# Where the sums of quarters for the two feed-forward output products are made

## The chip, the cores and the metric

The kernel runs on one core of a Trainium2 chip. The metric is device microseconds of that core, median of three runs. A core has five engines with a queue each, worked off in order: TensorE (PE in the profile; its weight loads are PEld), VectorE (DVE), ScalarE (ACT), GpSimd (POOL) and SyncE (SP), which here only issues transfers. A wait at the head of a queue holds everything behind it.

## The reference

Two transformer blocks run one after the other on a sequence of 1024 tokens of width 1024. Each ends with a feed-forward part, of which the part in question is the second product:

```python
# first block (D_FF = 3072), second block (FFN_HIDDEN = 2816)
x = x + (jax.nn.gelu(gate) * val) @ w_down[l]
x = x + (jax.nn.silu(gate) * up) @ w_ffn_out[l]
```

All is float32. The remaining parts (attention, recurrences, convolutions, norms, the first feed-forward products) are not touched.

## The kernel before

Activations are kept transposed, 128 channels on the partitions and 1024 tokens along the row. A float32 product is made of three matmuls on split operands, high by high, low by high and high by low (`mm3`, L389), where the high part is a rounded copy and the low part what the rounding left.

Each second product is computed by Strassen's scheme of seven half-size products. The hidden dimension is taken in pairs of 128 rows (12 pairs in the first block, 11 in the second); a pair has two weight tiles `wa`, `wb` and two activation tiles `ga`, `gb`, each 128x1024, loaded by SP from DRAM (`load`, L1837; all four show as `fs` in the profile). Every tile has a lower and an upper half. The seven products need sums and differences of halves, made in place or in the tiles `s` (weights) and `t` (activations): `sums` (L1846) writes `s1 = wa_lo - wa_hi`, `wa_hi += wb_hi`, `s0 = wa_hi - wa_lo`, `t1 = gb_hi - ga_hi`, `ga_hi -= ga_lo`, `t0 = gb_hi - ga_hi`, `t2 = gb_lo - t0`. An eighth, `s2 = wb_lo - s0`, is made later, in `down`'s inner function `operands`. All are TENSOR_TENSOR of 128x512 by the helper at L1542.

`down` (L1894) runs the work as a list of steps: groups of three pairs (the last group of the second block has two), within a group the seven products in turn, within a product the pairs. That gives 84 steps in the first block and 77 in the second. A step is 12 matmuls into four accumulator tiles `pd`. Three steps ahead of its matmuls a step's operands are prepared (`operands`, L1861): ScalarE rounds the weight half to `whi` (L384), writes `-whi` into `wlo` (L385), and a transfer issued by GpSimd adds the weight half to it (L386, `accum_op`); ScalarE rounds the activation half (L378) and VectorE subtracts (L379). The buffers `hi`/`lo` are four deep, so ScalarE starts on step x+3 when TensorE has left step x-1.

When the three pairs of a product are done, its four `pd` tiles are added to `acc` or to the residual tiles by VectorE (L1542, `add` L1872), two after the next step and two after the one behind that, before TensorE may use those accumulators again. The table `due` says behind which step the sums of a pair stand; a pair four ahead is loaded when its buffers come free. The engines' order is that of the code.

Of the kernel before, what the change touches and what calls it, by code (L numbers as in the profile page):

```python
# [16 lines left out]
ALU = mybir.AluOpType  # L17
# [3 lines left out]
S = 1024  # L21
# [3 lines left out]
H = 512  # L25
# [66 lines left out]
class Rope:  # L92
# [38 lines left out]
    def rstd(self, sums, n, post=None):  # L131

        nc, net = self.nc, self.net
        f = net.rt.unsqueeze(2).to_broadcast([P, 8, n])
        m = self.tp.tile([P, 8, n], F32, tag=f"qm{n}", name="qm")
        nc.vector.tensor_tensor(m, sums.rearrange("p (b n) -> p b n", n=n), f, op=ALU.mult)
        nc.vector.tensor_tensor(m, m, f, op=ALU.mult)
        r = net.rstd_small(m.rearrange("p b n -> p (b n)"), 8 * n, 1.0 / 64, EPS)
        rv = r.rearrange("p (b n) -> p b n", n=n)
        if post is None:  # L140
            nc.vector.tensor_tensor(rv, rv, f, op=ALU.mult)
        else:
            nc.vector.scalar_tensor_tensor(rv, rv, post, f, op0=ALU.mult, op1=ALU.mult)
        return r

    def sums(self, sq, n):
        pst = self.net.psT.tile([P, H], F32, tag="T", name="pst")
        self.net.colsum(pst, sq, self.net.ind[n], nb=8)
        return self.rstd(pst[:, 0:8 * n], n, 0.125 if n == 4 else None)
# [1373 lines left out]
class Ffn:  # L1523
# [17 lines left out]
    def tt(self, e, o, x, y, op=ALU.add):  # L1541
        e.tensor_tensor(o, x, y, op=op)  # L1542
# [303 lines left out]
    def sums(self, k):  # L1846

        t = self.raw[k]
        v, p, lo, hi = self.nc.vector, self.nc.gpsimd, slice(0, H), slice(H, S)
        sub = lambda e, o, x, y: self.tt(e, o, x, y, ALU.subtract)  # L1850
        t["s"], t["t"] = self.tile("s", k), self.tile("t", k)
        s, q, wa, wb, ga, gb = [t[n] for n in ("s", "t", "wa", "wb", "ga", "gb")]
        sub(v, s[:, 1], wa[:, lo], wa[:, hi])
        self.tt(p, wa[:, hi], wa[:, hi], wb[:, hi])
        sub(p, s[:, 0], wa[:, hi], wa[:, lo])
        sub(v, q[:, 1], gb[:, hi], ga[:, hi])
        sub(v, ga[:, hi], ga[:, hi], ga[:, lo])
        sub(v, q[:, 0], gb[:, hi], ga[:, hi])
        sub(v, q[:, 2], gb[:, lo], q[:, 0])

    def operands(self, i, k):  # L1861
        t, net = self.raw[k], self.net
# [23 lines left out]
    def down(self, dp, last, end):  # L1886
        nc, net = self.nc, self.net
        lo, hi = slice(0, H), slice(H, S)
# [29 lines left out]
        residual((0, 1, 2, 3))  # L1918
        self.load(3, "wa", "ga", "gb", "wb")
        due = [(0, 0), (1, 1), (2, 2), (9, 3)]  # L1920
        summed = set()

        def sums(k):
            if k not in summed:
                summed.add(k)
                self.sums(k)

        def operands(x):
            g, i, k = steps[x]
            if i not in (0, 2):  # L1930
                sums(k)
            self.operands(i, k)
            if i == (2 if g else 4):
                t = self.raw[k]
                self.tt(nc.gpsimd, t["s"][:, 2], t["wb"][:, lo], t["s"][:, 0], ALU.subtract)
            if k + 4 < n:
                if i == 4:
                    self.load(k + 4, "ga", "wa")
                elif i == orders[g][-1]:
                    self.load(k + 4, "gb", "wb")  # L1940
                    due.append((max(x - look + 2, due[-1][0] + 3 if due else 0), k + 4))

        for x in range(look):
            operands(x)
# [43 lines left out]
        for x, (g, i, k) in enumerate(steps[:len(steps) - rest]):  # L1988
            if g == len(groups) - 1 or g == 0 and i == 2:
                for f in adds:  # L1990
                    f()
                adds = []
            if x + look < len(steps):
                operands(x + look)
            for f in hooks.get(x - 0.5, ()):
                f()
            h, l = self.ready.pop(0)
            b, first = self.DOWN[i][4:]
            if k == groups[g][0] and first:
                banks[b] = [net.psB.tile([P, H], F32, tag="B", name="pd") for _ in range(4)]  # L2000
            for q in range(4):
                qs = slice(q * P, (q + 1) * P)
                net.mm3(banks[b][q], [((h[:, qs], l[:, qs]), (h[:, hi], l[:, hi]))],
                        first and k == groups[g][0], k == groups[g][-1], not first)
            for f in adds[:2]:
                f()
            del adds[:2]
            for f in hooks.get(x, ()):
                f()
            if due and due[0][0] <= x:  # L2010
                sums(due.pop(0)[1])
            if k == groups[g][-1]:
                for f in adds:
                    f()
                adds = self.add(banks[b], acc, g, i)
# [686 lines left out]
def ffn_plan(up, down, nf):  # L2702
    return pair_plan([up[i] for i in range(2 * nf)]) + [(f"sd{i}", down[i * P:(i + 1) * P, :]) for i in range(nf)]
# [149 lines left out]
```

## Time and profile before

| | us |
|---|---|
| median of three runs (3649.17 to 3652.49) | 3649.85 |
| the profiled execution | 3642.82 |
| its span, first to last instruction | 3641.0 |
| first block's second product, first to last `pd` matmul | 1045.3 to 1338.1 |
| second block's | 3357.0 to 3620.5 |

Over the whole span PE is busy 92%, DVE 69%, ACT 46%, POOL 50%. A matmul of 512 columns shows about 0.39 us, but the next begins about 0.23 us after it, so PE reads as busy also where it could go no faster. [...] An idle time stands in brackets with what ended it.

### The profile page before, as it was taken

How to read it: one execution, taken by the hardware profiler on the slowest of the kernel's cores; microseconds unless marked ns; L12 is line 12 of the kernel's file. 1: busy time of each engine (PE TensorE's matmuls, PEld its weight loads, DVE VectorE, ACT ScalarE, POOL GpSimd, SP SyncE). 2: the span in 40 equal slices, each digit the busy share in tenths (PEclk: the TensorE clock that was granted, in tenths of full speed). 3: DMA queues.
4: the chain of work that ended last, by engine and by line, in shares of the span. 5: the costliest groups of instructions: out<-in, count | busy, mean ns of one | idle time of the engine just before them, and what ended most of it. 6: DMA issues, size and time to landing. Idle time of an engine off the chain costs nothing. (4 is left out here: it accounts for less than half of the span.)

```text
span 3641.0 us, 42268 instructions
## 1 busy us (share of the span) xinstructions
PE 3341.6 (92%) x15494; PEld 2733.3 (75%) x15494; DVE 2516.3 (69%) x3033; ACT 1672.5 (46%) x2783; POOL 1813.2 (50%) x1216
## 2 busy tenths in 40 slices
PE   8788997999988988999999999999999989999897
PEld 6668885888867776777787886777777768887675
DVE  7888838667777898888877765756477662223877
ACT  5447823444445554444444553535433233333555
POOL 3434308999954552111111127876543287775544
PEclk9889998999999999999999999999999999999998
DMA  3131131222267742222222212333555312224874
GB/s 110 38 104 53 59 116 47 87 82 81 81 195 182 187 119 73 67 67 67 67 68 67 63 63 93 133 122 122 198 184 188 128 62 81 81 82 141 214 162 110
DMA packets 127808, 386.31 MB, mean 106 GB/s; under 512 B 16016, under 2 KB 16272, under 8 KB 127600
## 3 DMA queue, kind: packets, MB, share of 16 engines
q1 hardware_dynamic: 92144, 297.58, 24.9%
q0 software_dynamic: 28400, 61.12, 8.1%
q10 hardware_dynamic: 7056, 24.91, 1.7%
q8 instruction: 122, 2.00, 0.2%
q14 instruction: 86, 0.70, 0.1%
HBM read 232.25 MB, written 84.97 MB: 87 GB/s over the span
## 5 line engine op out<-in xcount | busy, mean ns | idle before, releaser
L379 POOL TENSOR_TENSOR wlo<-raw,whi 128x512 fp32r<-128x512 f32 (+1 forms) x266 | 476.8, 1802 | 789.0 <-ACT whi L378 772.0
L396 PE MATMUL pdn<-h,whi 128*128 128x512 f32 x1664 | 538.2, 404 | 16.8 <-DVE qb L1088 7.3
L1542 DVE TENSOR_TENSOR f<-pf,f 128x512 f32<-128x512 f32 x224 | 153.9, 688 | 365.6 <-PE pf L396 365.0
L378 ACT CAST whi<-raw 128x512 fp32r<-128x512 f32 (+1 forms) x283 | 206.7, 753 | 387.8 <-PE pf L396 166.2
L396 PEld LDWEIGHTS pdn<-h,whi 128*128 128x128 f32 x1664 | 316.7, 194 | 83.8 <-DVE qb L1088 10.2
L1042 DVE SCALAR_TENSOR_TENSOR cacc<-cu,vec,cacc 128x1024 f32<-128x1024 f32 x240 | 357.9, 1491 | 9.9 <-issue 2.2
L396 PE MATMUL pdn<-h,wlo 128*128 128x512 f32 x832 | 333.2, 400 | 0.0
L396 PE MATMUL pd<-whi 128*128 128x512 f32 x644 | 264.1, 410 | 40.1 <-DVE acc L1542 18.7
L396 PE MATMUL pd<-whi,wlo 128*128 128x512 f32 x644 | 264.1, 410 | 25.3 <-DMA wlo<-fs 17.7
L396 PE MATMUL pd<-wlo,whi 128*128 128x512 f32 x644 | 262.4, 407 | 0.0
L378 ACT CAST whi<-sb 128x512 fp32r<-128x512 f32 x128 | 79.1, 619 | 341.8 <-PE pf L396 259.9
L379 POOL TENSOR_TENSOR wlo<-sb,whi 128x512 fp32r<-128x512 f32 x128 | 173.0, 1356 | 105.7 <-ACT whi L378 105.4
L379 POOL TENSOR_TENSOR wlo<-sa,whi 128x1024 fp32r<-128x1024 f32 x64 | 177.9, 2779 | 54.0 <-ACT whi L378 53.8
L396 PE MATMUL pf<-h,whi 128*128 128x512 f32 x576 | 183.5, 400 | 10.6 <-ACT a L2463 5.6
L396 PEld LDWEIGHTS pdn<-h,wlo 128*128 128x128 f32 x832 | 161.1, 194 | 34.2
L396 PEld LDWEIGHTS pd<-whi 128*128 128x128 f32 x644 | 128.2, 199 | 70.7 <-issue 21.3
L396 PEld LDWEIGHTS pd<-whi,wlo 128*128 128x128 f32 x644 | 127.9, 199 | 61.5 <-DMA wlo<-fs 23.1
L396 PE MATMUL pp<-h,whi 128*128 128x512 f32 x448 | 150.3, 416 | 23.1 <-ACT h L532 10.0
L396 PEld LDWEIGHTS pd<-wlo,whi 128*128 128x128 f32 x644 | 127.8, 198 | 27.5
L386 POOL DMA_DIRECT2D wlo<-fs x92 | 84.8, 945 | 127.2 <-ACT wlo L385 98.2
L396 PEld LDWEIGHTS pf<-h,whi 128*128 128x128 f32 x576 | 109.3, 192 | 38.0 <-ACT a L2463 6.1
L1542 DVE TENSOR_TENSOR g<-pf,g 128x512 f32<-128x512 f32 x93 | 63.3, 685 | 104.5 <-PE pf L396 93.4
(564 smaller groups left out, 9714.2 us busy)
## 6 DMA issues: line engine op xcount, KB each, us to landing
raw<-in_w_in_dram SPq DMA_DIRECT2D x102, 512.0 KB, 3.5
raw<-in_w_up_dram SPq DMA_DIRECT2D x48, 512.0 KB, 3.5
gd<-f ACTq DMA_DIRECT2D x46, 512.0 KB, 2.6
fs<-gd SPq DMA_DIRECT2D x46, 512.0 KB, 6.5
wlo<-fs POOLq DMA_DIRECT2D x92, 256.0 KB, 4.3
raw<-in_w_ffn_in_dram SPq DMA_DIRECT2D x44, 512.0 KB, 3.5
wlo<-s POOLq DMA_DIRECT2D x69, 256.0 KB, 3.9
fs<-in_w_down_dram SPq DMA_DIRECT2D x24, 512.0 KB, 6.1
```

The lines of the kernel that those rows point to most:

```text
L378: (copy or self.nc.scalar.copy)(hi, src)
L379: (eng or self.nc.vector).tensor_tensor(lo, src, hi.bitcast(F32), op=ALU.subtract)
L386: nc.gpsimd.dma_start(lo.bitcast(F32), src, accum_op=ALU.add)
L396: nc.tensor.matmul(out, a, b, start=(first and i == 0), stop=(last and i == n - 1), skip_group_check=cont)
L1042: conv.append(lambda k=k: nc.vector.scalar_tensor_tensor(acc, u[:, k:k + S], cw(k), acc, op0=ALU.mult, op1=ALU.add))
L1542: e.tensor_tensor(o, x, y, op=op)
```

## The change

`sums` no longer issues its seven instructions at once; it returns them as a list, all on VectorE. The two that GpSimd made (`wa_hi += wb_hi` and `s0`) are now the second and third on VectorE. `down` takes up to three of them behind a step (four in the first six steps) instead of seven behind one. `s2` is made by VectorE too, right behind the low part that is subtracted in the same step. In this stage GpSimd is left with its transfers (and a few instructions of the two ends, which stay).

```diff
@@ -1846,17 +1846,14 @@
     def sums(self, k):
 
         t = self.raw[k]
-        v, p, lo, hi = self.nc.vector, self.nc.gpsimd, slice(0, H), slice(H, S)
-        sub = lambda e, o, x, y: self.tt(e, o, x, y, ALU.subtract)
+        lo, hi = slice(0, H), slice(H, S)
         t["s"], t["t"] = self.tile("s", k), self.tile("t", k)
         s, q, wa, wb, ga, gb = [t[n] for n in ("s", "t", "wa", "wb", "ga", "gb")]
-        sub(v, s[:, 1], wa[:, lo], wa[:, hi])
-        self.tt(p, wa[:, hi], wa[:, hi], wb[:, hi])
-        sub(p, s[:, 0], wa[:, hi], wa[:, lo])
-        sub(v, q[:, 1], gb[:, hi], ga[:, hi])
-        sub(v, ga[:, hi], ga[:, hi], ga[:, lo])
-        sub(v, q[:, 0], gb[:, hi], ga[:, hi])
-        sub(v, q[:, 2], gb[:, lo], q[:, 0])
+        tt = lambda o, x, y, op=ALU.subtract: lambda: self.tt(self.nc.vector, o, x, y, op)
+        return [tt(s[:, 1], wa[:, lo], wa[:, hi]), tt(wa[:, hi], wa[:, hi], wb[:, hi], ALU.add),
+                tt(s[:, 0], wa[:, hi], wa[:, lo]), tt(q[:, 1], gb[:, hi], ga[:, hi]),
+                tt(ga[:, hi], ga[:, hi], ga[:, lo]), tt(q[:, 0], gb[:, hi], ga[:, hi]),
+                tt(q[:, 2], gb[:, lo], q[:, 0])]
 
     def operands(self, i, k):
         t, net = self.raw[k], self.net
@@ -1918,12 +1915,15 @@
         residual((0, 1, 2, 3))
         self.load(3, "wa", "ga", "gb", "wb")
         due = [(0, 0), (1, 1), (2, 2), (9, 3)]
-        summed = set()
-
-        def sums(k):
-            if k not in summed:
-                summed.add(k)
-                self.sums(k)
+        left = {}
+
+        def sums(k, count=99):
+
+            if k not in left:
+                left[k] = self.sums(k)
+            while left[k] and count:
+                left[k].pop(0)()
+                count -= 1
 
         def operands(x):
             g, i, k = steps[x]
@@ -1932,7 +1932,7 @@
             self.operands(i, k)
             if i == (2 if g else 4):
                 t = self.raw[k]
-                self.tt(nc.gpsimd, t["s"][:, 2], t["wb"][:, lo], t["s"][:, 0], ALU.subtract)
+                self.tt(nc.vector, t["s"][:, 2], t["wb"][:, lo], t["s"][:, 0], ALU.subtract)
             if k + 4 < n:
                 if i == 4:
                     self.load(k + 4, "ga", "wa")
@@ -2007,8 +2007,14 @@
             del adds[:2]
             for f in hooks.get(x, ()):
                 f()
-            if due and due[0][0] <= x:
-                sums(due.pop(0)[1])
+            room = 4 if x < 6 else 3
+            while due and due[0][0] <= x and room:
+                k2 = due[0][1]
+                have = len(left[k2]) if k2 in left else 7
+                sums(k2, room)
+                room = max(room - have, 0)
+                if not left[k2]:
+                    due.pop(0)
             if k == groups[g][-1]:
                 for f in adds:
                     f()
```

The order of instructions shows the move. On GpSimd, at the first change of groups in the first block (`fs` are weight halves, `s` sums of pairs; DMA is the adding transfer), before and now:

```order
-L1542 TENSOR_TENSOR fs_8482<-fs_8482,fs_8688 128x512
-L1542 TENSOR_TENSOR s_8846<-fs_8482 128x512
 L386 DMA wlo<-fs_8194 128x512
-L1542 TENSOR_TENSOR s_8199<-fs_8194,s_8199 128x512
 L386 DMA wlo<-fs_8638 128x512
-L1542 TENSOR_TENSOR s_8702<-fs_8638,s_8702 128x512
 L386 DMA wlo<-fs_8663 128x512
-L1542 TENSOR_TENSOR s_8772<-fs_8663,s_8772 128x512
 L386 DMA wlo<-s_8199 128x512
```

Five instructions between the transfers are gone. On VectorE at the same place (`wlo` is the low part of an activation half, `acc<-pd` the addition of a finished product that TensorE waits for):

```order
+L1542 TENSOR_TENSOR s_8846<-fs_8482 128x512
+L379 TENSOR_TENSOR wlo<-fs_8193,whi 128x512
+L1542 TENSOR_TENSOR s_8199<-fs_8194,s_8199 128x512
+L1542 TENSOR_TENSOR acc_8195<-pd,acc_8195 128x512
+L1542 TENSOR_TENSOR acc_8196<-pd,acc_8196 128x512
 L1542 TENSOR_TENSOR t_8847<-fs_8686,fs_8480 128x512
 L1542 TENSOR_TENSOR fs_8480<-fs_8480 128x512
 L1542 TENSOR_TENSOR t_8847<-fs_8686,fs_8480 128x512
-L1542 TENSOR_TENSOR t_8847<-fs_8686,t_8847 128x512
-L379 TENSOR_TENSOR wlo<-fs_8193,whi 128x512
-L1542 TENSOR_TENSOR acc_8195<-pd,acc_8195 128x512
-L1542 TENSOR_TENSOR acc_8196<-pd,acc_8196 128x512
```

The low part and the first two additions now stand ahead of the activation sums of that pair, where all of its sums stood ahead of them; an `s2` has come in between. Earlier on VectorE, at the sums of the first pair that is loaded during the stage (`fs_8638` is its `wb`, the last of its four loads):

```order
 L1542 TENSOR_TENSOR s_8702<-fs_8416 128x512
+L1542 TENSOR_TENSOR fs_8416<-fs_8416,fs_8638 128x512
+L1542 TENSOR_TENSOR s_8702<-fs_8416 128x512
+L379 TENSOR_TENSOR wlo<-fs_8192,whi 128x512
+L1542 TENSOR_TENSOR f_8220<-pd,f_8220 128x512
+L1542 TENSOR_TENSOR f_8222<-pd,f_8222 128x512
```

VectorE's second instruction now reads `wb`, and a low part and two additions are queued behind it. The orders of TensorE, ScalarE and SyncE are as they were.

## Rows read from the trace of the kernel before

**Rows 1.** Windows, `pd` matmuls alone, of the two stages: us; busy (x) of PE, PEld, DVE, ACT; PEclk, DMA share, GB/s.

```profile
1045.32:1338.06 292.74, 249.48 (x1008) 198.28 (x1007) 65.87 (x104) 2.04 (x4) 0.92 0.72 180
3357.02:3620.51 263.49, 227.56 (x924) 181.84 (x923) 67.95 (x107) 2.04 (x4) 0.94 0.69 167
```

**Rows 2.** Timeline of PE, full and half clock: start, us, instruction.

```profile
1049.65 0.39 PE L396 MATMUL pd<-wlo,whi 128*128 128x512 f32 x1
1049.88 0.39 PE L396 MATMUL pd<-whi,wlo 128*128 128x512 f32 x1
...
1155.63 0.63 PE L396 MATMUL pd<-wlo,whi 128*128 128x512 f32 x1
1156.06 0.63 PE L396 MATMUL pd<-whi,wlo 128*128 128x512 f32 x1
```

**Rows 3.** Waits of PE, first block's stage, then second's: total us, times, longest.

```profile
PE pd L396 <- DMA wlo<-fs: 10.1, 6, 3.9
PE pd L396 <- DVE acc L1542: 9.3, 2, 5.1
PE pd L396 <- DVE f L1542: 8.1, 2, 7.5
PE pd L396 <- DMA wlo<-s: 3.6, 3, 2.0
...
PE pd L396 <- DVE acc L1542: 9.5, 2, 5.3
PE pd L396 <- DMA wlo<-fs: 7.6, 5, 2.8
PE pd L396 <- DMA wlo<-s: 4.0, 3, 2.4
```

**Rows 4.** Timeline of DVE, at the first change of groups.

```profile
1147.28 6.44 DVE L1542 TENSOR_TENSOR t<-fs,t 128x512 f32<-128x512 f32 x1
...
1154.24 1.27 DVE L1542 TENSOR_TENSOR acc<-pd,acc 128x512 f32<-128x512 f32 x2
```

**Rows 5.** Timeline of POOL, same place.

```profile
1147.23 1.61 POOL L1542 TENSOR_TENSOR s<-fs,s 128x512 f32<-128x512 f32 x1
...
1150.90 2.26 POOL L1542 TENSOR_TENSOR s<-fs,s 128x512 f32<-128x512 f32 x1
```

**Rows 6.** Windows behind two changes of groups; columns as in 1, with POOL.

```profile
1155.06:1157.99 2.93, 2.93 (x7) 2.36 (x8) 2.93 (x6) 0.00 (x0) 0.00 (x0) 0.50 0.35 62
1221.87:1226.25 4.38, 4.38 (x10) 3.44 (x11) 4.38 (x8) 0.00 (x0) 0.00 (x0) 0.50 0.23 42
```

**Rows 7.** Timelines of ACT, POOL and PE, a transfer issued late.

```profile
1121.30 0.63 ACT L385 ACTIVATE wlo<-whi 128x512 fp32r<-128x512 f32 x1
...
1125.91 2.67 POOL L386 DMA_DIRECT2D wlo<-fs  x3
...
1133.11 0.50 PE L396 MATMUL pd<-whi,wlo 128*128 128x512 f32 x1 [3.87 <-DMA wlo<-fs]
```

**Rows 8.** Timeline of DVE, sums of a pair while POOL computes nothing.

```profile
1120.37 0.68 DVE L1542 TENSOR_TENSOR s<-fs 128x512 f32<-128x512 f32 x1
1120.97 0.68 DVE L1542 TENSOR_TENSOR t<-fs,fs 128x512 f32<-128x512 f32 x1
1121.69 0.69 DVE L1542 TENSOR_TENSOR fs<-fs 128x512 f32<-128x512 f32 x1
```

**Rows 9.** Timeline of POOL, the pair's second sum; then DVE, 36 us earlier.

```profile
1122.76 1.50 POOL L1542 TENSOR_TENSOR fs<-fs,fs 128x512 f32<-128x512 f32 x1 [2.38 <-DMA fs<-in_w_down_dram]
...
1085.12 4.64 DVE L379 TENSOR_TENSOR wlo<-fs,whi 128x512 fp32r<-128x512 f32 x1 [2.22 <-ACT whi L378]
```

**Rows 10.** Source L386, first stage: POOL's issues, ns min/median/max.

```profile
L386 POOL DMA_DIRECT2D wlo<-s x36: 870/870/1896, 1067.1 to 1321.1; - x36
```

**Rows 11.** Windows, all instructions: PE, PEld, DVE, ACT, POOL, PEclk, DMA share, GB/s.

```profile
1045.00:1100.00 55.00, 40.34 (x147) 31.10 (x146) 45.10 (x46) 25.88 (x43) 27.72 (x24) 0.84 0.87 265
3350.00:3400.00 50.00, 43.70 (x176) 34.74 (x175) 37.41 (x42) 26.61 (x46) 27.33 (x24) 0.93 0.98 290
```

## The prediction

> **What bounds the kernel now.** First the windows of the two stages. The first block's second product takes 292.74 us for 1008 matmuls, the second block's 263.49 us for 924 [rows 1]. At full clock a matmul begins 0.227 us after the one before [rows 2], so TensorE alone would need 1008 x 0.227 = 228.8 and 924 x 0.227 = 209.7 us. The rest, 63.9 + 53.8 = 117.7 us, is all that any change here can win. At half clock the spacing is 0.425 us [rows 2], so 1 - 0.227/0.425 = 47% of a busy half-clock stretch is lost.
>
> Then the waits of TensorE, to see who ends them [rows 3]: transfers of `wlo`, VectorE's additions of finished products (`acc`, `f`). Third, the timelines of VectorE and GpSimd at such a wait. At the first change of groups a VectorE sum that reads two SBUF tiles, 0.69 us elsewhere in this stage [rows 8], takes 6.44 us, and the additions that TensorE needs stand behind it [rows 4]. In just that time GpSimd makes its three `s2` and issues transfers between them: 1147.23 to 1150.90 + 2.26 = 1153.16, and VectorE's sum ends at 1153.72 [rows 4, 5]. So a VectorE instruction with two SBUF operands stands while GpSimd computes, and not for one instruction only but until GpSimd has no more. TensorE gets its accumulator at the end of that: 9.3 us in two waits in the first stage, 9.5 in two in the second [rows 3].
>
> Last, the transfers: ScalarE had a `wlo` ready at 1121.30 + 0.63 = 1121.93, GpSimd issued its transfer at 1125.91 because two sums stood ahead of it, and TensorE waited 3.87 us for it [rows 7].
>
> **What goes, term by term.** The sums are made against the profiled execution of 3642.82 us.
>
> (A) Changes of groups, two in each stage. Without GpSimd sums nothing can hold VectorE's: 9.3 + 9.5 = 18.8 us of waits [rows 3]. Behind each the clock was at half for 2.93 to 4.38 us [rows 6], four times, some 3.6 each, of which 47% counts: 6.8. Together 25.6 us. What is late next is VectorE itself. In the nine steps ahead of the product that reads the accumulators it has three pairs' sums (three spacings of 0.60 and four of 0.72 where one reads what the last wrote [rows 8]: 4.7 each, 14.1), nine low parts at 0.60 (5.4), twelve additions at 0.60 (7.2) and two `s2` (1.2): 27.9 us, against 9 x 12 x 0.227 = 24.5 us of TensorE. It ends 3.4 us behind. The third accumulator's addition stands in the last of these steps. Counted from TensorE's start on the step before, that step begins at 2.7, ScalarE's three instructions take 2.0, low part, `s2` and addition 1.9, the lag so far 3.2: 9.8 us, where TensorE wants it three and a half steps on, at 9.5: a wait of 0.3. If `wb` lands late (below) up to 2 us. No row shows this burst, so the bounds are 0 and all 4.7 of the present mean wait; I take 1.0, near the arithmetic, four times. A = 25.6 - 4.0 = 21.6.
>
> (B) Late transfers outside the first group. The longest waits, 3.87 [rows 7] and 2.8 [rows 3], stand at the first change of groups of each stage, both with a half-clock stretch of 3.4 us behind them, 1.6 each. Issued about 4 us earlier, at once behind ScalarE, the transfer lands about 4 earlier if only the issue was late, and no earlier if the DMA engines are the limit. The next two transfers, issued back to back, land close behind and leave about 1.1 each. Of the smaller waits within the 10.1 and 7.6 [rows 3] I count 1.5. B = 3.87 + 2.8 + 3.2 - 2.2 + 1.5 = 9.2; bounds 0 and 11.4.
>
> (C) First group, first stage. Here a low part took 4.64 us behind GpSimd [rows 9] and TensorE waited 7.5 for an addition behind it [rows 3]; a late transfer cost 2.0 more [rows 3]. VectorE and ScalarE also finish the gelu of the last pair in this stretch, in one chain that the change doesn't shorten, so only about 4 of the 7.5 can go, with 2.0 and a half clock of about 1: 7. But the stretch ran at 87% of the DMA engines [rows 11]. Bounds 0 and 14; I take 5.
>
> (D) First group, second stage: two late transfers, 2.4 (the longest for `s` [rows 3]) and about as much for `fs`, and two half clocks at 1.6: 8 us at most. The DMA engines are at 98% there [rows 11]; I take 2.5.
>
> Sum: 21.6 + 9.2 + 5 + 2.5 = 38.3 us; 3642.8 - 38.3 = 3604.5 for the profiled execution. The median of the runs is 7.0 above it, so the forecast is 3649.85 - 38.3 = 3611.5, say 3611.
>
> **What it adds.** 69 instructions on VectorE (three for each of 23 pairs), 0.65 us each or 45 us, in stages where its sums stood still for longer than that; they delay TensorE only through (A). The low parts stay ahead of the sums in each step and are wanted three steps, 8.2 us, after TensorE begins the step that issues them; VectorE starts them about 2 us in, so a lag of 3.4 leaves 2 to spare. GpSimd gets no wait that it didn't have. The one new wait is VectorE's, for `wb`: its second sum stands behind that load, with a low part, two additions and the rest queued behind it and TensorE behind these. Now GpSimd bears it: 2.38 us where a pair four ahead is first summed [rows 9]. VectorE reaches that point about when it does now, so about 1.7 us, in a queue that then has over 2 us to spare for low parts; it is the "up to 2" of (A). ScalarE waits for `s0` a little earlier or later, at nothing: it stands on the buffers that TensorE frees.
>
> [...] An issue of GpSimd's takes 0.870 us in the median of 36 [rows 10], though VectorE subtracts two SBUF tiles in every step beside them. [...]
>
> **Rivals.**
> 1. *The transfers set the pace.* For: 87% and 98% of the DMA engines in the first groups [rows 11], loads and adding transfers share them, and a faster TensorE asks for them sooner. Against: over the whole stages 72% and 69% [rows 1]. Then B, C and D come to about a fifth, A stays: 21.6 + 3 = 25 us, 3625. Chance 0.19.
> 2. *VectorE becomes the bound at the changes of groups.* For: 27.9 against 24.5 us. Against: it needs a lag of 6 us, not 3.4, to wait as long as now. Then A is 5, the rest stays at 16.7: 21.7, or 3628. Chance 0.14.
> 3. *Slower: VectorE stands behind `wb`.* 15 pairs are loaded during the stages. From the point at which the load lands about 3 us after VectorE gets there, each further us goes through the additions to TensorE. Landing 7 us late: 15 x 4 = 60 us against 38 won, 3672. For: the present in-order GpSimd does wait there [rows 9]. Against: once with 2.38, the others less. Chance 0.06.
> 4. *No change*: TensorE gets to the next late thing (loads, half clock) and gives all back, 3648. Against: the four waits of A are ended by VectorE and not by a transfer. Chance 0.06.
>
> **How the numbers follow.** Forecast 0.55. It reaches from 3591 (A without residue, B, C and D at their upper bounds: 25.6 + 11.4 + 14 + 8 = 59) to 3635 (15 us left). The range for 8 in 10 takes in rivals 1 and 2 and reaches toward no change, with 3 us below for half-clock stretches not counted: 3588 to 3644. 0.2% is 7 us, about what a measurement here can tell from none. Faster: 0.55 + 0.19 + 0.14 less a little of each: 0.87. Same: 0.07. Slower: 0.06.
>
> **What would show it.** (A) no VectorE sum over 1 us until GpSimd's own instructions of the ending, and the two waits "DVE acc" of each stage at 0 to 2 us each; still 4 to 5 would be rival 2. (B, C, D) GpSimd's issue about 0.3 us behind ScalarE's `wlo` in every step; if that holds and TensorE still waits for `wlo`, rival 1. Rival 3: VectorE idle until the load of weights, above 3 us. PEclk of the stages up from 0.92 and 0.94 [rows 1] to about 0.97. The forecast is wrong if the two stages together shorten by under 15 or over 65 us, or if another stage changes by more than a few us, since nothing outside these two is touched.

## The result, and the profile after

The changed kernel takes 3603.30 us (median of four runs, 3594.54 to 3604.66) against 3649.78 before: 0.9866 of the time [0.9849, 0.9883], 46.5 us less. The forecast was 3611, 38.3 less. The profiled executions stand at 3603.38 and 3642.82, 39.4 apart. Windows of the two stages, `pd` matmuls alone; columns as in [rows 1], which they answer:

```profile
1049.26:1319.35 270.09, 242.59 (x1008) 193.06 (x1007) 66.07 (x104) 2.04 (x4) 0.95 0.79 195
3337.69:3580.85 243.16, 220.22 (x924) 175.92 (x923) 68.03 (x107) 2.04 (x4) 0.97 0.74 181
```

The stages are 22.65 and 20.33 us shorter, 43.0 together. Of the rest, 4.0 were lost ahead of the first stage (it begins at 1049.3 instead of 1045.3) in code that is the same in both.

Waits of TensorE in the first stage (1044 to 1335, total us, times, longest), answering [rows 3]:

```profile
PE pd L396 <- DMA wlo<-fs: 5.9, 6, 1.6
PE pd L396 <- DVE f L1542: 4.9, 2, 3.0
PE pd L396 <- ACT acc L1875: 3.7, 1, 3.7
PE pd L396 <- DMA wlo<-s: 2.4, 4, 0.9
...
PE pd L396 <- DVE acc L1542: 1.2, 1, 1.2
```

and in the second (3335 to 3602):

```profile
PE pd L396 <- DVE f L1542: 5.9, 1, 5.9
PE pd L396 <- DMA wlo<-fs: 4.3, 5, 1.5
...
PE pd L396 <- DVE acc L1542: 1.6, 1, 1.6
PE pd L396 <- DMA wlo<-s: 1.6, 3, 0.9
```

`DVE acc` falls from 9.3 and 9.5 us to 1.2 and 1.6; the longest wait for a transfer from 3.9 and 2.8 to 1.6 and 1.5. No half-clock stretch is left between the first and the last steps. Windows from the last one at the beginning to the first one at the end, same columns, PEclk (the share of TensorE's full clock that was granted) third from the right:

```profile
1097.90:1302.60 204.70, 195.32 (x847) 157.68 (x845) 59.76 (x94) 0.00 (x0) 1.00 0.81 193
3354.10:3552.00 197.90, 186.38 (x806) 149.92 (x804) 58.55 (x92) 0.00 (x0) 1.00 0.79 188
```

The first change of groups on VectorE, answering [rows 4]: nothing takes over 0.69 us, and the sums stand on both sides of the additions.

```profile
1145.12 0.68 DVE L1542 TENSOR_TENSOR t<-fs,fs 128x512 f32<-128x512 f32 x1
1145.83 0.69 DVE L1542 TENSOR_TENSOR fs<-fs 128x512 f32<-128x512 f32 x1
1146.56 0.69 DVE L1542 TENSOR_TENSOR t<-fs,fs 128x512 f32<-128x512 f32 x1
1147.17 0.68 DVE L379 TENSOR_TENSOR wlo<-fs,whi 128x512 fp32r<-128x512 f32 x1
1147.77 0.69 DVE L1542 TENSOR_TENSOR s<-fs,s 128x512 f32<-128x512 f32 x1
1148.37 1.28 DVE L1542 TENSOR_TENSOR acc<-pd,acc 128x512 f32<-128x512 f32 x2
```

TensorE's one wait there is for the first of these two additions (`acc` 2), the third accumulator, as the arithmetic of (A) had it:

```profile
1149.11 0.50 PE L396 MATMUL pd<-whi 128*128 128x512 f32 x1 [1.20 <-DVE acc L1542]
```

The transfer of [rows 7] is now issued 0.30 us behind ScalarE (1121.01 + 0.63 = 1121.64) instead of 3.98. Timelines of ACT, POOL and PE:

```profile
1121.01 0.63 ACT L385 ACTIVATE wlo<-whi 128x512 fp32r<-128x512 f32 x1
...
1121.94 0.87 POOL L386 DMA_DIRECT2D wlo<-fs  x1 [2.53 <-ACT wlo L385]
...
1130.36 0.50 PE L396 MATMUL pd<-whi,wlo 128*128 128x512 f32 x1 [1.43 <-DMA wlo<-fs]
```

The new wait that the prediction priced, VectorE's for `wb`, is there, longer than the 1.7 us it was given (timeline of DVE; the second stage has one of 3.6):

```profile
1123.56 0.69 DVE L1542 TENSOR_TENSOR fs<-fs,fs 128x512 f32<-128x512 f32 x1 [3.48 <-DMA fs<-in_w_down_dram]
```

The stages by parts, between the first matmuls of the steps named, counted in the two traces (us):

| steps | prediction's term | first stage | second stage | won |
|---|---|---|---|---|
| 0 to 16 | C, D | 72.41 to 67.50 | 62.10 to 56.37 | 4.9 + 5.7 |
| 17 to 23 | B | 24.87 to 21.46 | 23.73 to 20.81 | 3.4 + 2.9 |
| 24 to 62 | A, and small waits of B | 123.87 to 111.46 | 122.83 to 111.23 | 12.4 + 11.6 |
| 63 on | none | 71.59 to 69.67 | 54.83 to 54.76 | 1.9 + 0.1 |

### The profile page after: what moved, and what is told of

Its sections match the earlier page's. It is cut to its first block, busy times and chain, and to the rows that moved or that the text cites. A ratio compares the mean times of both kernels' runs of the same rounds, so it can differ in the third digit from the quotient of the medians.

```text
span 3601.6 us, 42275 instructions
## 1 busy us (share of the span) xinstructions
PE 3326.7 (92%) x15494; PEld 2722.3 (76%) x15494; DVE 2485.1 (69%) x3102; ACT 1673.1 (46%) x2783; POOL 1709.3 (47%) x1147
## 3 DMA queue, kind: packets, MB, share of 16 engines
q1 hardware_dynamic: 92144, 297.58, 25.3%
## 5 line engine op out<-in xcount | busy, mean ns | idle before, releaser
L386 POOL DMA_DIRECT2D wlo<-fs x92 | 79.9, 871 | 192.8 <-ACT wlo L385 138.8
```

The source lines that it names most:

```text
L386: nc.gpsimd.dma_start(lo.bitcast(F32), src, accum_op=ALU.add)
```

## The experiments

Each was timed beside the kernel before in the same set of runs. Its ratio goes with the median; the stages' lengths are from one profiled execution each. They are steadier than the whole time (last section), but not exact: in the first stage, steps 0 to 16 of the changed kernel take 67.50 us and those of the kernel with the endings on VectorE, whose code up to there is the same, 64.55. "Stages" is the sum of both: 556.2 us before, 513.3 in the changed kernel.

| edit | median us | ratio to before | stages us |
|---|---|---|---|
| the change | 3603.3 | 0.9866 [0.9849, 0.9883] | 513.3 |
| `s2` back on GpSimd | 3613.7 | 0.9903 [0.9889, 0.9918] | 530.5 |
| the two other sums back | 3610.1 | 0.9899 [0.9882, 0.9915] | 523.6 |
| all on VectorE, seven at once | 3595.1 | 0.9857 [0.9843, 0.9871] | 514.3 |
| spread, GpSimd keeps its three | 3638.9 | 0.9973 [0.9961, 0.9984] | 548.8 |
| endings on VectorE | 3589.6 | 0.9850 [0.9835, 0.9865] | 504.4 |
| additions first | 3595.3 | 0.9856 [0.9843, 0.9870] | 509.5 |
| copies early, ten low parts direct | 3588.8 | 0.9841 [0.9826, 0.9856] | 504.2 |
| all of these | 3567.7 | 0.9791 [0.9776, 0.9807] | 486.3 |
| the same, sixteen direct | 3568.1 | 0.9780 [0.9763, 0.9797] | 485.4 |
| the same, all direct | 3598.6 | 0.9860 [0.9843, 0.9877] | 511.3 |

**Spreading or moving?**

```diff
# all on VectorE, seven at once
-            room = 4 if x < 6 else 3
+            room = 7
```

> The changed kernel with all seven sums of a pair behind one step instead of three or four a step, all on VectorE. Theory (taking GpSimd's instructions away is what won): the same 27.9 us in nine steps, only in lumps of 4.7 us against a step of 2.7, so the waits for acc grow by 0 to 2 us each: 3603 to 3611. Rival (spreading is what won): VectorE's lumps stand ahead of the additions at each change of groups and term A, some 21 us, is lost: about 3625.

The stages are 1.1 us longer, the ratio lies within the change's interval. The median lies 8 us below the expected range. TensorE waits 2.2 and 2.0 us for `acc` instead of 1.2 and 1.6. With all sums on VectorE, spreading is worth nothing in the sum: it saves 5.7 us in steps 17 to 62 and loses as much in steps 0 to 16.

```diff
# spread, GpSimd keeps its three
-tt(wa[:, hi], wa[:, hi], wb[:, hi], ALU.add)
+tt(wa[:, hi], wa[:, hi], wb[:, hi], ALU.add, e=p)      # p = nc.gpsimd
# and likewise s0 and s2
```

> The kernel before with the spreading alone: three or four sums a step, but GpSimd still makes wa_hi += wb_hi, s0 and s2. Theory (taking GpSimd's instructions away is what won): VectorE is still held at each change of groups and transfers are still issued late, 3638 to 3652 beside 3650 of the kernel before. Rival (spreading is what won): most of the 46 us is there, 3603 to 3620.

36 of the 43 us are gone again. The 7 that are left (548.8 against 556.2, and a ratio whose interval stays below 1) are what spreading wins as long as GpSimd keeps its sums. Timelines of DVE and POOL at the first change of groups:

```profile
1149.33 6.37 DVE L1542 TENSOR_TENSOR fs<-fs 128x512 f32<-128x512 f32 x1
...
1149.20 1.62 POOL L1542 TENSOR_TENSOR s<-fs,s 128x512 f32<-128x512 f32 x1
1150.43 1.24 POOL L386 DMA_DIRECT2D wlo<-fs  x1
1151.03 1.96 POOL L1542 TENSOR_TENSOR s<-fs,s 128x512 f32<-128x512 f32 x1
1152.27 1.57 POOL L386 DMA_DIRECT2D wlo<-fs  x1
1152.86 2.28 POOL L1542 TENSOR_TENSOR s<-fs,s 128x512 f32<-128x512 f32 x1
```

Another VectorE sum than in [rows 4], and held for the same 6.4 us, until GpSimd's three are done: 1155.70 against 1155.14. So what is held is what happens to stand there.

**Which of GpSimd's sums?**

```diff
# s2 back on GpSimd
-self.tt(nc.vector, t["s"][:, 2], t["wb"][:, lo], t["s"][:, 0], ALU.subtract)
+self.tt(nc.gpsimd, t["s"][:, 2], t["wb"][:, lo], t["s"][:, 0], ALU.subtract)
```

> The changed kernel (3603.3 us) with s2 alone back on GpSimd: three GpSimd sums at each change of groups, everything else as in the changed kernel. Theory (a VectorE instruction on two SBUF tiles stands while GpSimd computes): the waits for acc come back. If GpSimd makes its three s2 back to back as before, VectorE is held about 6 us and the time rises by the 16 us of waits and 7 of half clock, to about 3625. If they now come one a step, since the two other sums no longer hold GpSimd up, each hold is about 1.6 us and the rise is a few us at each of the four changes, 8 to 14 us in all, to 3611 to 3617. Rival (GpSimd's computing does not hold VectorE; what won was the spreading and the earlier issues): 1.2 us less on VectorE at each change, 3601 to 3605.

It went by the theory's second case, but dearer: the stages are 17.2 us longer (the median 10 to 14). DVE and POOL:

```profile
1138.30 2.58 DVE L379 TENSOR_TENSOR wlo<-t,whi 128x512 fp32r<-128x512 f32 x1
1140.80 2.60 DVE L1542 TENSOR_TENSOR s<-fs 128x512 f32<-128x512 f32 x1
1143.43 0.69 DVE L1542 TENSOR_TENSOR fs<-fs,fs 128x512 f32<-128x512 f32 x1
1144.15 1.94 DVE L1542 TENSOR_TENSOR s<-fs 128x512 f32<-128x512 f32 x1
...
1138.67 1.64 POOL L1542 TENSOR_TENSOR s<-fs,s 128x512 f32<-128x512 f32 x1
...
1141.21 1.62 POOL L1542 TENSOR_TENSOR s<-fs,s 128x512 f32<-128x512 f32 x1
...
1143.95 1.58 POOL L1542 TENSOR_TENSOR s<-fs,s 128x512 f32<-128x512 f32 x1
```

One hold for each `s2`, of 1.9 to 2.6 us, each ending 0.6 us behind GpSimd's instruction. With three 1.6 us instructions VectorE loses 1.9 + 1.9 + 1.3 = 5.1 us against 0.69 each.

```diff
# the two other sums back on GpSimd
-tt(wa[:, hi], wa[:, hi], wb[:, hi], ALU.add), tt(s[:, 0], wa[:, hi], wa[:, lo])
+tt(wa[:, hi], wa[:, hi], wb[:, hi], ALU.add, e=p), tt(s[:, 0], wa[:, hi], wa[:, lo], e=p)
```

> The changed kernel with wa_hi += wb_hi and s0 back on GpSimd (46 GpSimd instructions of some 1.5 us), s2 and the other sums on VectorE, spread as in the changed kernel. Theory: transfers are issued late again where GpSimd waits for a wb load or computes ahead of them, so terms B and C come back, 9 to 15 us, to 3612 to 3618; VectorE sums beside GpSimd's take 1.5 to 3 us instead of 0.7, and the waits for acc may grow. Rival (transfers set the pace, a late issue costs nothing): 3603 to 3606, with TensorE's waits for wlo as in the changed kernel though the issues are 2 to 4 us late.

3610.1, or 3613 by the ratio; stages 10.3 us longer. No wait for `acc` is left at all, VectorE having 46 instructions fewer, but the waits for transfers grow from 8.3 to 12.7 us in the first stage and from 5.9 to 8.3 in the second. The longest in the first stage (PE), and POOL ahead of it: two sums, then a pair of issues at once.

```profile
1096.33 1.29 POOL L1542 TENSOR_TENSOR fs<-fs,fs 128x512 f32<-128x512 f32 x1 [2.17 <-DVE s L1542]
1097.69 1.63 POOL L1542 TENSOR_TENSOR s<-fs 128x512 f32<-128x512 f32 x1
1099.27 1.89 POOL L386 DMA_DIRECT2D wlo<-s  x2
...
1107.50 0.80 PE L396 MATMUL pd<-whi,wlo 128*128 128x512 f32 x1 [2.95 <-DMA wlo<-s]
```

At step 21, where the longest waits of term B stood, the same transfers are issued as late as in the kernel before: 4.1 us behind ScalarE in the first stage and 3.4 in the second. Timelines of ACT, POOL and PE in the first:

```profile
1122.98 0.63 ACT L385 ACTIVATE wlo<-whi 128x512 fp32r<-128x512 f32 x1
...
1127.74 2.69 POOL L386 DMA_DIRECT2D wlo<-fs  x3
...
1132.41 0.50 PE L396 MATMUL pd<-whi,wlo 128*128 128x512 f32 x1 [1.51 <-DMA wlo<-fs]
```

TensorE waits 1.5 us here and not at all in the second stage: no more than in the changed kernel (1.4 and 1.5), which issues them at once. In these steps it went by the rival.

What each edit adds to the changed kernel's stages, by the parts of the table above (us, first + second stage):

| steps | `s2` back | the two others back | all three back |
|---|---|---|---|
| 0 to 16 | 0.6 + 1.1 | 3.6 + 5.1 | 6.3 + 3.4 |
| 17 to 23 | -1.4 + 0.2 | -0.6 - 0.8 | 2.8 + 3.1 |
| 24 to 62 | 9.0 + 7.7 | -0.5 - 0.4 | 9.3 + 9.4 |
| 63 on | -0.2 + 0.2 | 1.7 + 2.3 | 1.7 - 0.3 |

`s2` costs its 17.2 us in the steps of term A, the two others most of their 10.3 in those of C and D. All three cost 35.5, 8 more than the sum; the excess stands in steps 17 to 23, which neither edit alone makes longer. Why, no run here tells.

**Does the hold show where nothing was changed?** The endings still have GpSimd additions. Changed kernel, DVE and POOL in the second block's ending:

```profile
3544.76 3.45 DVE L1542 TENSOR_TENSOR f<-f,acc 128x512 f32<-128x512 f32 x1
...
3553.09 2.47 DVE L1542 TENSOR_TENSOR f<-pd,f 128x512 f32<-128x512 f32 x4
...
3544.80 2.85 POOL L1542 TENSOR_TENSOR f<-f,acc 128x512 f32<-128x512 f32 x2
...
3553.81 1.60 POOL L1542 TENSOR_TENSOR f<-f,acc 128x512 f32<-128x512 f32 x1
```

A sum of two SBUF tiles is held for 3.45 us over GpSimd's two; four additions whose one operand is an accumulator `pd` in PSUM run at 0.6 each beside GpSimd's third.

```diff
# endings on VectorE
-self.tt(nc.gpsimd if m == 2 and q % 2 else nc.vector, o, o, acc[q])
+self.tt(nc.vector, o, o, acc[q])
# and the additions of squares (sd) of both endings likewise
```

> The changed kernel with the GpSimd additions of the two endings (the shares f <- f,acc of the second block's last group, and the sums of squares sd of both endings) on VectorE too, in the same places. Theory (a VectorE instruction on two SBUF tiles stands while GpSimd computes, and what stands behind it waits too): the second block's ending has VectorE instructions of 2.2 to 3.8 us beside GpSimd's; they fall to 0.7, and TensorE's wait of 6.06 us for f at that stage's step 71 falls to 0 to 3; the time to 3593 to 3600. Rival (these waits belong to the chain of the ending itself, and VectorE with some ten instructions more is later): 3603 to 3608, with the 6.06 as it is.

3589.6, or 3595 by the ratio. The last part of the second stage goes from 54.76 to 48.09 us, the wait for `f` at step 71 from 6.06 to 2.5, for ScalarE. DVE there, each addition at 0.6 to 0.7:

```profile
3535.28 1.29 DVE L1542 TENSOR_TENSOR f<-f,acc 128x512 f32<-128x512 f32 x2
...
3539.48 1.89 DVE L1542 TENSOR_TENSOR f<-f,acc 128x512 f32<-128x512 f32 x3
```

**What holds the changed kernel now?**

```diff
# additions first
+            for f in adds[:2]:
+                f()
+            del adds[:2]
             if x + look < len(steps):
                 operands(x + look)
...
-            for f in adds[:2]:          # behind the step's matmuls
-                f()
-            del adds[:2]
```

> The changed kernel with the two additions of a finished product ahead of a step's low part and s2 on VectorE, where they stood behind them. Theory (VectorE is late at the change of groups by what stands ahead of the third addition in its step): the waits of 1.36 and 1.80 us for acc go to 0 to 0.3, 3598 to 3601 if nothing else moves. Rival (the lag is that of the whole burst): the waits stay above 1 us, 3602 to 3605.

The wait for `acc` is gone in the first stage and 0.8 in the second (1.2 and 1.6): the order within the step was most of the residue. The median lies 3 us below the expected range, but the ratio's interval overlaps the change's, so the time alone doesn't tell the two apart.

```diff
# copies early, ten low parts direct
+            if x == m0 - 1:              # last step of the first product, after its matmuls
+                for f in self.add(banks[b], acc, g, i):
+                    f()
+                operands(x + look)
...
-        net.split_dma(h[:, lo], l[:, lo], t[an][:, ax])
+        (net.split if direct else net.split_dma)(h[:, lo], l[:, lo], t[an][:, ax])
```

> The changed kernel with two edits on waits that it has left. First, ScalarE's four copies of the first product into acc stand ahead of the operands of step 5 instead of behind them: the waits of 3.84 and 3.49 us at step 3 should go to about 0.5, and the half-clock stretch behind each. Second, in steps 2, 9, 13, 15, 21, 35, 36, 40, 41 and 62 VectorE subtracts the weight half as well, without a transfer: if the 0.4 to 1.7 us that TensorE still waits for wlo there are the 7 to 8 us in which a transfer lands (the issue stands 0.3 us behind ScalarE), they go to 0, some 5 us in each stage. By both: 3582 to 3592. Rival (the operands themselves are late, since ScalarE starts them when TensorE frees the buffers, and the clock or the next late transfer takes it back): 3597 to 3605.

Within its range, by a mixture. The waits in the ten steps are gone, and the 3.84 and 3.49 us for the copies. In place of the latter stand waits for the transfer of the same step 3, 4.30 and 3.38 us, and new ones at steps 10, 14 and 56 (1.3 to 2.4). Stages: 9.1 us less.

```diff
# all of these, and
-            room = 4 if x < 6 else 3
+            room = 7 if x < 10 else 3
```

> The edits of the three other kernels of this set together, and seven sums behind a step in the first ten steps. If they act on different waits their gains add: 10 to 30 us under the changed kernel, 3573 to 3593. If VectorE, with the sums of both endings and ten low parts more, is the next bound: 3595 to 3603, with its waits for acc and f above 2 us.

3567.7 us beats both kernels; the stages lose 26.9 us, where the three apart lose 8.9 + 3.7 + 9.1 = 21.7: the gains add. The 5 us more do not stand where the early sums act: up to step 23 this kernel wins less than the three apart (6.2 against 11.3 us), and from step 63 on 7.5 more. No run tells why.

```diff
# sixteen direct, then all
-self.operands(i, k, x in (2, 9, 13, 15, 21, 35, 36, 40, 41, 62))
+self.operands(i, k, x in (2, 3, 9, 10, 13, 14, 15, 21, 22, 35, 36, 40, 41, 56, 62, 63))
+self.operands(i, k, True)
```

> The kernel with all those edits (3567.7 us) with six steps more whose weight low part VectorE makes itself: 3, 10, 14, 22, 56, 63, where TensorE now waits 4.65, 4.76, 1.95, 0.97, 1.38 and 0.62 us in the first block and 4.19, 2.44, 1.30 and 0.43 in the second. If each wait is only the landing time of one transfer: 15 to 20 us less, 3547 to 3556. If these steps' operands are late themselves (a load of the raw tiles that lands late, buffers freed late), the next step's wait takes its place as it did when steps 2, 9, 13 and 21 were taken: 3560 to 3568. If VectorE is the bound by now: above 3568, with waits for low parts made by VectorE.

No gain, as the second case had it. Waits of TensorE in the first stage:

```profile
PE pd L396 <- DMA wlo<-fs: 10.9, 2, 7.1
```

There were six for transfers (11.5 and 1.8 us); two are left, at the next steps with a transfer (4 and 11), and longer. In the first group, where the DMA share of the kernel with ten was 0.91 (1045 to 1100), taking transfers out handed the wait to the next one.

> The same kernel with no adding transfer left in the two stages: VectorE makes the low part of the weights too in all 161 steps, some 0.6 us more in each, and GpSimd is left with nothing there. In the nine steps ahead of a change of groups VectorE then has 27.9 + 9 x 0.6 = 33.3 us against TensorE's 24.5, so if VectorE's count is what bounds it, it falls about 9 us behind at each of the four changes and TensorE waits 5 to 6 us for acc at each, more than the transfers cost: 3575 to 3595. If low parts of three steps ahead give it enough room: 3545 to 3560.

3598.6, 4 us above the range that was expected if VectorE's count bounds; the stages at 511.3. Waits of TensorE in the first stage, and the stage's window:

```profile
PE pd L396 <- DVE f L1542: 10.6, 3, 6.3
PE pd L396 <- DVE wlo L379: 6.8, 6, 3.0
PE pd L396 <- DVE acc L1542: 3.7, 2, 1.8
...
1047.97:1318.60 270.63, 244.67 (x1008) 196.50 (x1007) 66.01 (x104) 2.35 (x4) 0.94 0.30 114
```

The DMA share is 0.30 against 0.79 in the changed kernel, and the waits listed are VectorE's. The expected place (`acc`) costs 1.8 each, not 5 to 6; the rest stands at the low parts and at `f`. So VectorE's count bounds once it has 0.6 us more in every step.

## Why the prediction was right

(A) was 21.6. The waits for `acc` fell from 18.8 to 2.8 us (residue forecast: 4.0) and the four half-clock stretches, 6.8, are gone: 22.8, and steps 24 to 62 shortened by 24.0 with the small waits of B in them. The mechanism is shown, not only its price: with all of GpSimd's sums back the hold returns at the same length on another VectorE instruction; with `s2` alone it returns in three pieces; with seven sums at once and no GpSimd sum it stays away. `s2` is what counts: back on GpSimd alone it lengthens steps 24 to 62 by 16.7 us, the two other sums by nothing. With `s2` alone on GpSimd each hold is of one instruction (1.9 to 2.6 us at the first change), but there are three at each change, and they add up. Spreading, half of the change's wording, wins 7 us while GpSimd keeps its sums and nothing once they are gone; the prediction gave it no term. One of its readings was too wide: VectorE's sums do not all take 0.69 us elsewhere in the stage [rows 8]; in the kernel before, `ga_hi -= ga_lo` took 1.64 in the median of its 12, beside GpSimd's two other sums. That changes no term of (A).

The residue stands at the third accumulator of the first change, as worked out, and none at the second. Its size was the arithmetic's upper case (1.36 and 1.80 between matmul starts against 0.3 to 2).

(B) was 9.2. The two longest waits fell by 2.4 and 1.3 in the profile's list (3.9 to 1.6 or less, 2.8 to 1.5) and their half-clock stretches are gone; steps 17 to 23 shortened by 6.3, forecast 3.87 + 2.8 + 3.2 - 2.2 = 7.7. So the size is about right, but the cause that the prediction gave, the late issue, is not borne out. The issue is 3.7 us earlier, but TensorE gets the transfer 8.4 us behind it (1130.36 - 1121.94), where that was 7.2 before; the residue of 1.1 each was 1.4 to 1.5. With the two other sums back on GpSimd the issues are late again, and the waits stay at 1.5 us and none, with steps 17 to 23 no longer than in the changed kernel: TensorE gets the transfer of the first stage 4.7 us behind its issue (1132.41 - 1127.74). So here the late issue cost nothing, as rival 1 had it. What shortened these steps stays open; their gain is lost only where GpSimd makes all three sums (2.8 + 3.1 us).

(C) was 5, measured 4.9; that it came so near is partly luck, as the same steps took 3 us less in another execution of the same code (64.55). The late transfers of steps 5 and 13 cost 0.5 us instead of 3.9 and the waits at step 9 fell from 8.1 to 5.9, but step 3 waits 2.4 longer. (D) was 2.5 and measured 5.7: the term that was mis-sized. The argument was that the DMA engines, at 98% [rows 11], would not let transfers land earlier. They did: of the three half-clock stretches of 3.4 us that stood there, one is left, and the waits for `wlo` fell with them. That GpSimd's two other sums matter in these steps is borne out: with them back, steps 0 to 16 are 3.6 and 5.1 us longer. In the first stage the issue of step 13 is 2.9 us late again and TensorE waits 2.95; in the second the issues of steps 4, 6 and 7 are 1.2 to 1.8 late, and ScalarE also stands 2.5 us for an `s0` that GpSimd makes, a wait that the prediction put at nothing.

Rival 2 (VectorE the bound) did not come about at this change, only when 0.6 us more a step was put on it. Rival 3 was nearer than thought: VectorE stood 3.5 and 3.6 us for `wb`, past the 3 us that the prediction set as the sign, but once in each stage and not for 15 pairs, and TensorE did not stop for it. Of the signs, no VectorE sum of halves took over 0.7 us until the endings, and GpSimd's issue came 0.3 to 0.5 us behind ScalarE in all but 6 of the 161 steps; TensorE still waits 14.2 us for `wlo` (25.3 before), so in part rival 1. PEclk reached 0.95 and 0.97 where about 0.97 was expected. "Nothing else changes by more than a few us" held only as far as executions agree on it.

The forecast fell 8 us short of the medians: 4.7 of it in the stages (43.0 against 38.3), the rest in the scatter of the untouched parts.

## What to carry to other kernels

If VectorE instructions with two SBUF operands take several times their usual length (6.44 us against 0.69 here), look at what GpSimd computes in that time, and price a GpSimd addition by what VectorE loses beside it (5.1 us for three here), not by GpSimd's idle time. Move the work to VectorE as long as its count in the tightest stretch fits, and leave GpSimd the transfers; whether the work is spread evenly matters less. A late issue need not be what a wait costs: issue it late again with the rest as it is, and look. After such a gain the waits for transfers come next, and taking six more away by one edit only handed them on here (the DMA share was 0.88 and 1.04 in the changed kernel's first 50 us or so of the two stages).

## What the runs showed of the hardware

At the places shown above the hold lasted as long as GpSimd's work: 6.37 and 6.44 us over three instructions with transfer issues between them, 3.45 over two, 1.9 to 2.6 over one `s2`. Beside three instructions VectorE did not get in between. Beside the two other sums it did: in the kernel before, at 1052 us, GpSimd's take 1.64 and 1.63 us and two of VectorE's 1.64 and 1.68, each ending 0.6 behind one of GpSimd's. Why the one and the other, no run here tells. VectorE's additions with one operand in PSUM were not held: 0.6 us each beside GpSimd's addition, and none of those with `pd` took over 0.69 in the two stages of the kernel before.

GpSimd's issues were not slowed by more VectorE work: median 872 ns in the changed kernel's first stage (`wlo<-fs` and `wlo<-s` alike) against 874 and 870 before.

Code that no edit touches varies from execution to execution: between the end of the first stage and the start of the second the twelve profiled kernels show 2002.8 to 2019.0 us, and up to the first stage 1045.3 to 1050.2. Two of the ratios above that differ by under 0.003 are not told apart by time, where the waits in the stages tell them apart, and the stages' lengths as far as they differ by more than the 3 us of steps 0 to 16.
